# Row-wise infinity norm on one core: the second load moves to the first load's queue, and the last store goes out in two halves

## The chip, the core and the metric

The kernel runs on one core of a Trainium2 chip. The metric is the device time of one execution in microseconds (us), and lower is better. Three runs of the kernel before gave 629.17, 629.47 and 629.51, a median of 629.47.

A core has several engines with an instruction stream each. Three compute here: VectorE (DVE in the profile), ScalarE (ACT) and GpSimd (POOL). SyncE (SP) computes nothing and issues transfers. A transfer between the device's memory (HBM) and the on-chip memory of 128 partitions is issued by SP or by ScalarE's queue (ACTq), and is carried out by 16 DMA engines, whichever queue it came from. When it has landed, a semaphore tells those that wait for it.

## The reference

```python
def setup_inputs():
    return {"x": np.random.randn(8192, 8192).astype(np.float32)}

def reference(x):
    return np.linalg.norm(x, ord=np.inf, axis=1)
```

`x` is two-dimensional and an axis is given, so the norm is that of each row as a vector: the largest absolute value of its 8192 elements. The input has 268.4 MB, the output 32 KB.

## The kernel before

**Layout.** The 8192 rows are split over the 128 partitions, 64 rows in each, in two groups (`GROUPS = [46, 18]`): in a group of k rows per partition a partition's rows lie one behind the other in HBM. Along the free dimension the kernel walks through the 64 rows as one strip of 64 x 8192 values. A result column of the tile `res` (128 x 64) belongs to each of the 64 rows.

**Loads.** The strip is read by 38 loads. The list `WHOLE` has 31 of 16384 values per partition (two rows, 64 KB per partition, 8.39 MB in all) and one of 8192. The list `LAST` cuts the last row into six pieces of 3920, 1984, 1040, 576, 320 and 352 values. All but the last piece go into `ring`, which holds three whole loads; the last has a tile of its own (`last`), behind whose values the partial results of the last row are put. A load into a part of the ring that is in use waits until the work on it is done, so load 4 has to wait for the reduce of load 1, load 5 for that of load 2, and so on. For half the loads the kernel also declares that the wait for the earlier load itself isn't needed, since the reduces in between imply it.

**Reduces.** For every whole load VectorE runs one reduce over two rows with the maximum of absolute values (line 68, in the helper `absmax`). Towards the end, in the loads that have widths in their second entry, the work on a row is shared (helper `shared`): VectorE takes the first part, ScalarE takes the absolute values of the others (line 90), and GpSimd takes their maximum (line 75, helper `max_pool`), on the bits as integers. Another `max_pool` or, for the last row, a last `absmax` over 361 columns puts the partial results together.

**Queues.** The helper `load` issues every load by SP, except for the second one (`len(loads) == 1`), which ScalarE's queue issues (line 110). ScalarE's first computing instruction (line 142) has no effect on the results; it comes after the second load's reduce, and brings its table load to the front of ScalarE's stream.

**Stores.** SP issues the last store (`final`, line 156): the column of the last row, 128 x 1 values. ScalarE's queue issues two earlier ones (line 161): 46 columns of the first group and 17 of the second. The call of `add_manual_dep` behind them sets the order in which two of the stores get their semaphores; it adds no wait. At the end SP waits until all transfers have landed (line 192), and all engines meet.

`keep` fixes the order of what passes through it; the rest is ordered by the tile framework along the dependencies.

Of the kernel before, what the change touches and what calls it, by code (L numbers as in the profile page):

```python
# [1 line left out]

# [4 lines left out]

P = 128
FP32 = mybir.dt.float32
INT32 = mybir.dt.int32  # L10
MAX = mybir.AluOpType.max
X = mybir.AxisListType.X
ABS = mybir.ActivationFunctionType.Abs

GROUPS = [46, 18]


WHOLE = (
    [(16384, ())] * 30 + [(16384, (3712, 3680)), (8192, (2016, 1984))]
)
LAST = [
    (3920, (1680,)), (1984, (848,)), (1040, (432,)), (576, (240,)), (320, ()), (352, ())
]
RING = 3 * 16384


@with_exitstack  # L30
def kernel(
    ctx: ExitStack,
    tc: tile.TileContext,
    x: bass.AP,
    out: bass.AP,
):
    nc = tc.nc
    n_rows, n_cols = x.shape
    R = n_rows // P
    assert R == sum(GROUPS) and n_cols == 8192  # L40
    keep = tc.keep_in_program_order


    first = []
    x_of, out_of = {}, {}
    for k in GROUPS:
        f = len(first)
        x_of[f] = x[f * P : (f + k) * P].rearrange("(p r) m -> p (r m)", r=k)
        out_of[f] = out[f * P : (f + k) * P].rearrange("(p r) -> p r", r=k)
        first += [f] * k  # L50

    single = ctx.enter_context(tc.tile_pool(name="single", bufs=1))

    ring = single.tile([P, RING], FP32)
    res = single.tile([P, R], FP32)

    n_parts = sum(1 + len(g) for w, g in LAST[:-1])
    last = single.tile([P, LAST[-1][0] + n_parts], FP32)

    def not_before(inst, other, why):  # L60
        tc.add_manual_dep(
            inst.ins, other.ins.name,
            mybir.DependencyInfo(mybir.DependencyClass.Sync, mybir.DependencyReason.DATA),
            reason=why,
        )

    def absmax(dst, src):
        return keep(nc.vector.tensor_reduce(  # L68
            out=dst, in_=src, axis=X, op=MAX, apply_absolute_value=True,
        ))  # L70

    def max_pool(dst, src):

        pool = nc.gpsimd
        keep(pool.add_instruction(  # L75
            mybir.InstTensorReduce(
                name=nc.get_next_instruction_name(),
                ins=[pool.lower_ap(src.bitcast(INT32))],
                outs=[pool.lower_ap(dst.bitcast(INT32))],
                op=MAX,  # L80
                axis=X,
            )
        ))

    def shared(part, buf, g):

        a = buf.shape[1] - sum(g)
        red = absmax(part[:, :1], buf[:, :a])
        for i, c in enumerate(g):
            keep(nc.scalar.activation(buf[:, a : a + c], buf[:, a : a + c], ABS))  # L90
            max_pool(part[:, 1 + i : 2 + i], buf[:, a : a + c])
            a += c
        return red

    loads = []

    def load(pos, w):

        row = pos // n_cols
        a = pos - first[row] * n_cols  # L100
        if pos + w == R * n_cols:
            buf = last[:, :w]
        else:
            at = loads[-1][0] + loads[-1][1] if loads else 0
            if at + w > RING:
                at = 0
            buf = ring[:, at : at + w]

        queue = nc.scalar if len(loads) == 1 else nc.sync
        inst = queue.dma_start(out=buf, in_=x_of[first[row]][:, a : a + w]).ins  # L110
        if pos + w < R * n_cols:
            if (len(loads) + 4) % 10 < 5:


                for b, v, earlier in loads:
                    if b < at + w and at < b + v:
                        tc.declare_no_dep(
                            inst, earlier, reason="ordered by the reduces in between",
                        )
            loads.append((at, w, inst))  # L120
        return buf


    pos = 0
    for u, (w, g) in enumerate(WHOLE):
        buf = load(pos, w)
        row, k = pos // n_cols, w // n_cols
        pos += w
        whole = k - 1 if g else k
        if whole:  # L130
            red = absmax(
                res[:, row : row + whole],
                buf[:, : whole * n_cols].rearrange("p (c m) -> p c m", m=n_cols),
            )
        if g:
            part = single.tile([P, 1 + len(g)], FP32, name=f"part{u}")
            shared(part, buf[:, whole * n_cols :], g)
            max_pool(res[:, row + whole : row + k], part)
        if u == 1:

            not_before(
                keep(nc.scalar.activation(res[:, :1], res[:, :1], ABS)),  # L142
                red, "not before the second row is in",
            )


    n = LAST[-1][0]
    for h, (w, g) in enumerate(LAST[:-1]):
        buf = load(pos, w)
        pos += w  # L150
        shared(last[:, n : n + 1 + len(g)], buf, g)
        n += 1 + len(g)

    load(pos, LAST[-1][0])
    absmax(res[:, R - 1 :], last)
    final = nc.sync.dma_start(out=out_of[first[-1]][:, GROUPS[-1] - 1 :], in_=res[:, R - 1 :])


    for f, o in out_of.items():
        k = min(o.shape[1], R - 1 - f)  # L160
        early = keep(nc.scalar.dma_start(out=o[:, :k], in_=res[:, f : f + k]))
    tc.add_manual_dep(
        early.ins, final.ins.name,
        mybir.DependencyInfo(mybir.DependencyClass.NoSync, mybir.DependencyReason.SCHED_ONLY),
        reason="takes the later semaphore",
    )


# [1 line left out]
_INS = ['x']  # L170
_OUTS = [((8192,), 'float32')]


# [23 lines left out]
```

## Time and profile before

| | |
|---|---|
| runs of the kernel before | 629.17, 629.47, 629.51 us |
| the profiled execution, its own time | 629.51 us |
| its span in the profile | 627.7 us |
| HBM read, mean rate over the span | 268.44 MB, 428 GB/s |
| VectorE, wait for the first load | 41.9 us |
| VectorE, waits for loads in all | 89.2 us in 24 waits |
| SP's queue, share of 16 DMA engines | 260.05 MB, 96.0% |
| ScalarE's queue, share of 16 DMA engines | 8.42 MB, 3.1% |
| one reduce of a whole load, x31 with its other form | 16.94 us on average |

The span runs from the first to the last record of the profiled execution; its own time is 1.8 us longer. Engines are counted as busy while they compute, and the issue of a transfer isn't counted. A wait of VectorE for a load isn't a loss in itself where the DMA engines have no pause. The time to landing of a transfer counts from its issue and holds the time in which it stands in the queue behind others.

### The profile page before, as it was taken

The page shows a single profiled execution, that of the slowest core. Times are in us where ns is not written, and L with a number is a line of the kernel's source. Part 1 is how long each engine was busy: PE and PEld are TensorE (multiplying, and loading weights), DVE is VectorE, ACT ScalarE, POOL GpSimd, SP SyncE. Part 2 cuts the span into 40 slices and gives each one's busy share as a digit, 9 for nine tenths or more (in the row PEclk, how much of TensorE's full clock was granted, in tenths as well). Part 3 has the DMA queues.
Part 4 walks back from the last instruction along what each step waited for, and adds up shares of the span by engine and source line. Part 5 has one row for each costly group of instructions (what it writes and reads, how often), then busy time and mean ns, then how long its engine had stood idle before and what let it go on. Part 6 is the DMA issues. An engine that isn't in the chain of part 4 may idle for free.

```text
span 627.7 us, 173 instructions
## 1 busy us (share of the span) xinstructions
DVE 535.8 (85%) x39; ACT 15.0 (2%) x10; POOL 14.1 (2%) x14
## 2 busy tenths in 40 slices
DVE  0039999999998898888998888988889888899888
ACT  0000000000000000000000000000000000000044
POOL 0000000000000000000000000000000000000026
DMA  9999999999999999999999999999999999999996
GB/s 401 409 459 401 434 430 438 430 438 430 434 434 426 443 418 451 413 455 409 459 409 459 409 459 405 464 405 464 405 464 405 459 409 455 413 451 418 451 407 280
DMA packets 5904, 268.47 MB, mean 428 GB/s; under 512 B 1040, under 2 KB 1296, under 8 KB 1680
## 3 DMA queue, kind: packets, MB, share of 16 engines
q1 hardware_dynamic: 5472, 260.05, 96.0%
q10 hardware_dynamic: 432, 8.42, 3.1%
HBM read 268.44 MB, written 0.03 MB: 428 GB/s over the span
## 4 chain that ended last, share of the span: by engine, by line
DMA 57%; DVE 42%; issue 0%; SPq 0%; DVEq 0%
DMA ring<-in_x_dram 57%; DVE res L68 41%; DVE last L68 1%; SPq L110 0%; DVEq L68 0%
## 5 line engine op out<-in xcount | busy, mean ns | idle before, releaser
L68 DVE TENSOR_REDUCE res<-ring 128x2 f32<-128x16384 f32 (+1 forms) x31 | 524.6, 16942 | 89.2 <-DMA ring<-in_x_dram 89.2
L90 ACT ACTIVATE ring<-ring 128x3712 f32<-128x3712 f32 (+7 forms) x8 | 13.6, 1718 | 534.3 <-DMA ring<-in_x_dram 534.2
L75 POOL TENSOR_REDUCE part<-ring 128x1 int32<-128x3712 int32 (+3 forms) x4 | 10.1, 2562 | 609.7 <-ACT ring L90 609.7
L68 DVE TENSOR_REDUCE part<-ring 128x1 f32<-128x800 f32 (+1 forms) x2 | 5.5, 2748 | 0.1
L68 DVE TENSOR_REDUCE last<-ring 128x1 f32<-128x2240 f32 (+4 forms) x5 | 5.3, 1115 | 0.2 <-DMA ring<-in_x_dram 0.2
L75 POOL TENSOR_REDUCE last<-ring 128x1 int32<-128x1680 int32 (+3 forms) x4 | 3.4, 854 | 0.6 <-ACT ring L90 0.4
L142 ACT ACTIVATE res<-res 128x1 f32<-128x1 f32 x1 | 0.2, 203 | 73.8 <-DVE res L68 73.8
L142 ACT ACT_TABLE_LOAD x1 | 1.3, 1283 | 1.2 <-PEq L181 1.2
L68 DVE TENSOR_REDUCE res<-last 128x1 f32<-128x361 f32 x1 | 0.5, 530 | 0.1
L75 POOL TENSOR_REDUCE res<-part 128x1 int32<-128x3 int32 x2 | 0.4, 197 | 0.1
L181 POOL MEMSET const-float32-0.0<- 128x1 f32 x1 | 0.1, 98 | 0.2 <-issue 0.2
L181 POOL MEMSET const-bfloat16-1.0<- 128x1 bf16 x1 | 0.1, 101 | 0.0
L181 POOL MEMSET const-uint8-127<- 128x1 uint8 x1 | 0.1, 101 | 0.0
L181 POOL MEMSET const-float32-1.0<- 128x1 f32 x1 | 0.1, 98 | 0.0
## 6 DMA issues: line engine op xcount, KB each, us to landing
ring<-in_x_dram SPq DMA_DIRECT2D x1, 4096.0 KB, 31.1
ring<-in_x_dram SPq DMA_DIRECT2D x1, 1960.0 KB, 35.4
ring<-in_x_dram SPq DMA_DIRECT2D x1, 992.0 KB, 37.4
ring<-in_x_dram SPq DMA_DIRECT2D x1, 520.0 KB, 38.2
ring<-in_x_dram SPq DMA_DIRECT2D x30, 40.8
ring<-in_x_dram SPq DMA_DIRECT2D x1, 288.0 KB, 38.4
last<-in_x_dram SPq DMA_DIRECT2D x1, 176.0 KB, 38.3
ring<-in_x_dram SPq DMA_DIRECT2D x1, 160.0 KB, 38.3
```

Source lines behind the costliest of these rows:

```text
L68: return keep(nc.vector.tensor_reduce(out=dst, in_=src, axis=X, op=MAX, apply_absolute_value=True,))
L75: keep(pool.add_instruction(mybir.InstTensorReduce(name=nc.get_next_instruction_name(), ins=[pool.lower_ap(src.bitcast(INT32))], outs=[poo ...
L90: keep(nc.scalar.activation(buf[:, a : a + c], buf[:, a : a + c], ABS))
L142: keep(nc.scalar.activation(res[:, :1], res[:, :1], ABS)),
L181: nc = _bacc.Bacc("TRN2", target_bir_lowering=False, num_devices=1)
```

## The change

The second load is issued by SP, as all others are, so the rule by which a queue was chosen is gone. The last store is cut at partition 64: the upper half of the partitions goes by ScalarE's queue, behind the two earlier stores, and the lower half by SP. Each half waits for the last reduce. The call that sets the order of the semaphores now stands between these two.

```diff
-        queue = nc.scalar if len(loads) == 1 else nc.sync
-        inst = queue.dma_start(out=buf, in_=x_of[first[row]][:, a : a + w]).ins
+        inst = nc.sync.dma_start(out=buf, in_=x_of[first[row]][:, a : a + w]).ins
...
     load(pos, LAST[-1][0])
     absmax(res[:, R - 1 :], last)
-    final = nc.sync.dma_start(out=out_of[first[-1]][:, GROUPS[-1] - 1 :], in_=res[:, R - 1 :])
+    for f, o in out_of.items():
+        k = min(o.shape[1], R - 1 - f)
+        keep(nc.scalar.dma_start(out=o[:, :k], in_=res[:, f : f + k]))
 
 
-    for f, o in out_of.items():
-        k = min(o.shape[1], R - 1 - f)
-        early = keep(nc.scalar.dma_start(out=o[:, :k], in_=res[:, f : f + k]))
+    half = P // 2
+    o = out_of[first[-1]][:, GROUPS[-1] - 1 :]
+    second = keep(nc.scalar.dma_start(out=o[half:], in_=res[half:, R - 1 :]))
     tc.add_manual_dep(
-        early.ins, final.ins.name,
+        nc.sync.dma_start(out=o[:half], in_=res[:half, R - 1 :]).ins, second.ins.name,
         mybir.DependencyInfo(mybir.DependencyClass.NoSync, mybir.DependencyReason.SCHED_ONLY),
         reason="takes the later semaphore",
     )
```

## The prediction

> **What bounds the kernel now.** I read the page first (engine shares, the chain that ended last), then the chain in order of time, then single DMA issues with their landing times, and last the tail. Loads are numbered from 1 in the order of the code; load 2 is the one that ScalarE's queue issues.
>
> ```profile
> DVE 535.8 (85%) x39; ACT 15.0 (2%) x10; POOL 14.1 (2%) x14
> DMA  9999999999999999999999999999999999999996
> DMA 57%; DVE 42%; issue 0%; SPq 0%; DVEq 0%
> ```
>
> VectorE (DVE) is free for 15% of the span, while the DMA engines show 90% or more in all slices but the last. So data arrival should set the pace, although the chain gives VectorE 42%. The chain in time tells why it does:
>
> ```profile
> 0.74 41.12 DMA ring<-in_x_dram
> ...
> 41.88 137.11 DVE res L68 x8
> ...
> 179.01 39.12 DMA ring<-in_x_dram
> ...
> 218.16 17.23 DVE res L68
> ...
> 276.21 17.23 DVE res L68
> ...
> 566.47 17.23 DVE res L68
> ```
>
> Columns are start, length, what. From 218.16 on the chain repeats one pattern, a reduce of 17.23 and a load of 40.79, and VectorE waits 2.13 us before each reduce. The pace there is (566.47 - 218.16) / 18 loads = 19.35 us for 8.39 MB, with loads always queued behind each other. This is the stream's own pace. Two more readings stand against it. First, loads 1 and 2 land together, 41.12 us after their issue, which is 2 x 19.35 + 2.42: the start of the stream costs 2.42, and VectorE can't begin until 41.88. Second, from the landing of load 2 (41.86) to that of load 11 (218.13) nine loads take 176.27 us; nine at 19.35 would take 174.15. About 2.12 us are lost in there, although VectorE, which was late, isn't what a stream needs, unless it releases a buffer late. It does so once. The three rows below are from three looks: the issues near the start, the first reuse of a buffer (timeline), and that issue's time to landing.
>
> ```profile
> 0.73 0.40 ACTq L110 DMA_DIRECT2D ring<-in_x_dram  x1
> 0.74 0.85 SPq L110 DMA_DIRECT2D ring<-in_x_dram  x2
> DMA to landing us min/median/max: 41.1/41.3/60.0
> ```
>
> ```profile
> 59.13 0.33 SPq L110 DMA_DIRECT2D ring<-in_x_dram  x1
> ```
>
> ```profile
> ring<-in_x_dram SPq DMA_DIRECT2D x1, 23.6
> ```
>
> Load 3 is issued at about 1.17 and lands 60.0 later, at 61.2. Load 4 overwrites load 1's buffer, so it waits for the first reduce and is issued at 59.13, when only 2.0 us of load 3 are left in the queue. It lands at 59.13 + 23.6 = 82.7, that is 21.5 us after load 3 and not 19.35. The stream ran dry here, or nearly, and had to start again: 82.73 - 61.17 - 19.35 = 2.2 us lost, all of what the chain misses (2.12). Later issues have more cover; by 179.01 it is 39.12 - 19.35 = 19.8 us of queued loads, and nothing more is lost.
>
> The tail still hangs on arrival:
>
> ```profile
> 605.17 8.69 DVE L68 TENSOR_REDUCE res<-ring 128x1 f32<-128x8192 f32 x1 [2.13 <-DMA ring<-in_x_dram]
> 619.56 5.27 DVE L68 TENSOR_REDUCE last<-ring 128x1 f32<-128x2240 f32 x5 [0.16 <-DMA ring<-in_x_dram]
> 624.93 0.53 DVE L68 TENSOR_REDUCE res<-last 128x1 f32<-128x361 f32 x1
> 625.49 0.35 SPq L156 DMA_DIRECT2D out_dram<-res  x1
> ```
>
> VectorE waited for a load just before 605.17 and again before 619.56; from there it runs on to the last reduce (ends 625.46), SP issues the last store at 625.49, and the span ends at 627.7. If all loads come earlier by some amount, the tail from 605.17 comes earlier by as much, since 2.13 us of waiting stand before it and all of that is for loads.
>
> **The change part by part.**
>
> *Load 2 from ScalarE's queue to SP's, behind load 1.* ScalarE's queue loses one issue of 0.40 us; its table load (1.28 us from 1.16) moves up to about 0.74 and hides in 70 us of idle time. SP gains one issue: 0.33 to 0.43 by its own rows, before load 3, which then goes out near 1.6 instead of 1.17. At that time load 1 has 20 us to run, which hides it; without that cover it would cost 0.4. No wait is added: in the built order the first three SP loads wait for nothing, and the later waits are the old ones with load 1's and load 2's semaphores exchanged.
>
> What it does to the stream: load 1's packets no longer share the engines with load 2's. Load 1 then lands at 0.74 + 2.42 + 19.35 = 22.5 and load 2 still near 41.9, for the bytes are the same. The first reduce runs from 22.5 to 39.8, and load 4 is issued at 39.8 instead of 59.13, with 61.2 - 39.8 = 21.4 us of loads ahead of it. The steady part has the same cover (40.79 - 19.35 = 21.4) and loses nothing, so the dry spot goes: -2.12 by the chain, -2.2 by the two landings; I take -2.17. Where that stall goes: VectorE starts 19.4 us earlier, works off no backlog, and waits about 2.1 us for each load from the start. Loads are late next, at their own pace, and that nobody speeds up here. The gain isn't 19.4 us since a VectorE that starts early only waits more.
>
> Bounds on this term. The new start is one queue's alone, which no row shows cold. The nearest rows are the cold start of the two queues (2.42 from issue) and load 4's lone issue, which lands 23.6 - 19.35 = 4.25 after it, 2.0 of them behind load 3. Were the whole 4.25 the price of a lone start, it would cost 4.25 - 2.42 = 1.8 and leave -0.35. The other end: a lone issue takes 0.33 instead of 0.38 and, without the second queue, the start might lose 0.3 less, giving -2.5. I stay at 2.42 because it is the only start from rest in the trace. A queue with three whole loads also is no new thing: before the end SP has eight loads issued and not landed (the issues up to 586.47 stand behind a load that lands near 605).
>
> *The last store in two halves.* One SP issue of 0.35 us and 128 rows becomes two issues of 64 rows, on SP and on ScalarE's queue, both waiting for the last reduce. ScalarE's half stands behind two stores that end at 624.32 + 0.44 = 624.77, 0.7 us before the reduce is done; behind it is only the engine's end. SP's half gets another earlier semaphore to wait for, that of the load reduced at 621.97, long landed. The rows for such a store:
>
> ```profile
> out_dram<-res ACTq DMA_DIRECT2D x1, 23.0 KB, 1.5
> out_dram<-res ACTq DMA_DIRECT2D x1, 8.5 KB, 1.5
> out_dram<-res SPq DMA_DIRECT2D x1, 0.5 KB, 1.4
> ```
>
> Forty-six times the bytes cost 0.1 us, so halving the bytes gains 0 to 0.1. Against it, ScalarE's rows are 0.1 longer than SP's, and two issues at once took 0.40 and 0.38 at the start where a lone one takes 0.33. If the second half's issue waits out the first it costs 0.35; if the halves go wholly one after the other, 1.4. I take +0.1, bounds -0.1 and +1.4, nearest to the pair at the start, whose landings (41.1 and 41.3) lie within 0.2.
>
> A rule of the Trainium skill speaks against this part: the page "DMA: Bandwidth & Descriptors", section "Rules for kernel authors", says not to split a transfer into two partition halves, because both use the same 16 engines and serialize. The rows above agree that loads share the engines, and leave open what it means for 256 bytes. With that page's fixed cost of about 2 us for a DMA (its section on the anatomy of a DMA, given there for another issuing path) a full serialization would be an estimated 629.3 in place of 627.4.
>
> Sum on the profiled execution: 629.51 - 2.17 + 0.1 = 627.44 (span 627.7 - 2.07 = 625.6, and 1.8 around it). The median of the runs shown is 629.47, 0.04 below that execution: 627.4.
>
> **The rivals.**
>
> *A slow lone start.* Load 1 lands near 24.3 instead of 22.5. For it: load 4's lone issue took 4.25. Against: part of that was spent behind load 3, and load 4 had to wait for engines still busy. Time: 629.47 - 0.35 + 0.1 = 629.2.
>
> *The halves serialize.* For it: the second store on ScalarE's queue needed 0.44 where the one ahead took 0.34. Against: the two loads at the start went on together. Time: 629.47 - 2.17 + 1.4 = 628.7.
>
> *The change doesn't do what it says*: load 1 lands no earlier because the engines take loads 1 and 2 in turn even from one queue, so load 4 still goes out near 59. Against it: from load 4 on each SP load lands 19.35 after the one before, never in pairs. Time: 629.47 + 0.1 = 629.6.
>
> *Slower: one late DMA engine.* A load is landed when the last of its engines is done, and engines that take their shares from one queue don't wait for each other. If the lone cold start leaves one of them behind, every later landing is behind by as much, to the end. It is priced at its lag, one for one; it makes the kernel slower than before from 2.07 us of lag beyond today's start, and measurably so from 2.07 + 1.26 = 3.3; with 3.6 it is 631.0. For it: the loss at load 4 stayed to the end. Against: both starts seen lie 1.8 apart at most.
>
> **How the numbers follow.** 0.2% is 1.26 us, about what a measurement of this kernel tells from no change: faster is below 628.21. Gap closed, 627.4: 0.74, by itself 626.9 to 628.0. Slow lone start, 629.2: 0.10, a third of it still under 628.21. Halves serialize, 628.7: 0.07, a quarter of it under. No effect, 629.6: 0.04. Late engine, 631.0: 0.05. Faster 0.74 + 0.03 + 0.02 = 0.79; slower 0.05 and 0.01 from the top of the no-effect case; same 0.15. Range 626.7 to 628.8: below, the -2.5 and a store gain of 0.1; above, up to the serialized halves.
>
> **What would show it.** First reduce near 22.5; load 4 issued near 40 and landing 19.35 after load 3, about 41 after its issue; a wait of 2.13 before each reduce from the second on; the last reduce ending near 623.3; two stores issued together, landing within 0.2 of each other about 1.5 later. Wrong would be a landing of load 1 past 24, any two loads over 20 us apart, or an end more than 2.4 us after the last reduce.

## The result, and the profile after

The changed kernel took 628.0 us (median of 6 runs, 627.92 to 628.12), the kernel before 630.0 (median of 6 runs: the three shown above, 629.17 to 629.51, and three beside the changed kernel, 630.49 to 631.1). The ratio is 0.9967 with a 95% interval of 0.9954 to 0.998: 0.33% faster, between 0.2% and 0.46%. Run again later against other runs of the kernel before, the changed kernel had a ratio of 0.9977 (0.9968 to 0.9986). The profiled execution took 627.92, with a span of 626.1 against 627.7.

The page of the changed kernel, engine shares and the chain that ended last:

```profile
DVE 536.5 (86%) x39; ACT 15.0 (2%) x10; POOL 14.1 (2%) x14
DMA 71%; DVE 28%; SPq 0%; issue 0%; DVEq 0%
```

VectorE does the same work in the same time, but the chain's share of it fell from 42% to 28%: the long stretch of eight reduces in a row, in which VectorE caught up, is gone. The same chain in order of time (start, length, what):

```profile
0.74 0.38 SPq L108
...
1.18 40.68 DMA ring<-in_x_dram
41.85 0.02 issue
41.88 17.23 DVE res L68
59.11 0.02 issue
59.12 40.79 DMA ring<-in_x_dram
...
564.36 17.23 DVE res L68
```

From 41.88 on, the pattern of one reduce and one load repeats to the end: (564.36 - 41.88) / 27 loads = 19.35 us, the stream's own pace, now without an exception. The timeline around the first reuse of a buffer, in rows from three windows:

```profile
22.56 17.22 DVE L68 TENSOR_REDUCE res<-ring 128x2 f32<-128x16384 f32 x1 [22.56 <-DMA ring<-in_x_dram]
39.80 0.33 SPq L108 DMA_DIRECT2D ring<-in_x_dram  x1
61.23 17.22 DVE L68 TENSOR_REDUCE res<-ring 128x2 f32<-128x16384 f32 x1 [2.13 <-DMA ring<-in_x_dram]
80.59 17.22 DVE L68 TENSOR_REDUCE res<-ring 128x2 f32<-128x16384 f32 x1 [2.15 <-DMA ring<-in_x_dram]
```

Load 1 is there at 22.56 instead of 41.88, load 4 goes out at 39.80 instead of 59.13, and the reduces of loads 3 and 4 (the last two rows) start 19.36 apart. Before, load 4 landed 21.5 after load 3.

The tail (timeline), and the last two stores' times from issue to landing:

```profile
617.44 5.28 DVE L68 TENSOR_REDUCE last<-ring 128x1 f32<-128x2240 f32 x5 [0.16 <-DMA ring<-in_x_dram]
622.82 0.53 DVE L68 TENSOR_REDUCE res<-last 128x1 f32<-128x361 f32 x1
623.38 0.53 SPq L163 DMA_DIRECT2D out_dram<-res  x1
623.38 0.54 ACTq L161 DMA_DIRECT2D out_dram<-res  x1
```

```profile
out_dram<-res SPq DMA_DIRECT2D x1, 0.2 KB, 1.7
out_dram<-res ACTq DMA_DIRECT2D x1, 0.2 KB, 2.0
```

The last reduce starts 2.11 us earlier than before (624.93), all of it won at the front. It ends at 623.35 and the span at 626.1: 2.8 us, where the kernel before needed 627.7 - 625.46 = 2.3. So the store gives 0.5 back. Each half takes 0.53 to issue, where the whole store took 0.35, and lands 1.7 and 2.0 later instead of 1.4. The sum, -2.1 + 0.5, is the -1.6 of the two spans.

### The profile page after: what moved, and what is told of

Read it like the earlier page. It is cut to its first block, busy times and chain, and to the rows that moved or that the text cites. A ratio compares the mean times of both kernels' runs of the same rounds, so it can differ in the third digit from the quotient of the medians.

```text
span 626.1 us, 174 instructions
## 1 busy us (share of the span) xinstructions
DVE 536.5 (86%) x39; ACT 15.0 (2%) x10; POOL 14.1 (2%) x14
## 4 chain that ended last, share of the span: by engine, by line
DMA 71%; DVE 28%; SPq 0%; issue 0%; DVEq 0%
DMA ring<-in_x_dram 71%; DVE res L68 28%; DVE last L68 1%; SPq L108 0%; DVEq L68 0%
```

## The experiments

Each is a kernel of its own; medians are given with the range of their runs. A ratio compares with runs of the kernel before on the same chip, taken together with the row's own. The first four rows share one chip, the next four another, and e5 and e6 a third.

| kernel | us, median (range) | ratio to before (95%) |
|---|---|---|
| load 2 by SP, old store (e1) | 627.52 (627.38 to 627.67) | 0.9973 (0.9963 to 0.9984) |
| load 2 by ScalarE, store in halves (e2) | 629.85 (629.04 to 630.38) | 1.0010 (1.0001 to 1.0019) |
| e1, load 4 held back until the second reduce is done (e3) | 629.28 (628.57 to 630.53) | 1.0005 (0.9997 to 1.0014) |
| before, load 4 in two pieces (e4) | 627.52 (627.37 to 627.69) | 0.9976 (0.9965 to 0.9986) |
| the changed kernel again (a1) | 628.02 (627.95 to 628.21) | 0.9977 (0.9968 to 0.9986) |
| e1, whole store by ScalarE's queue (s3) | 627.53 (627.33 to 627.57) | 0.9969 (0.9956 to 0.9981) |
| both halves by SP (s4) | 628.45 (628.31 to 628.58) | 0.9985 (0.9976 to 0.9994) |
| e1, 17 columns stored beside the last store (s5) | 627.77 (627.64 to 628.22) | 0.9973 (0.9964 to 0.9983) |
| e1, load 4 held back until half of the second reduce is done (e5) | 627.50 (627.38 to 627.69) | 0.9970 (0.9958 to 0.9983) |
| e1, load 4 held back until 15/16 of the second reduce are done (e6) | 628.05 (627.62 to 629.50) | 0.9980 (0.9971 to 0.9989) |

Two more kernels, s6 and s7, ran once each, on the chip of e5 and e6, for the issue times in their profiles; their total times are not used.

### The two parts alone (e1, e2)

e1 keeps the load part and restores the old store; e2 keeps `nc.scalar if len(loads) == 1 else nc.sync` and has the new store.

```diff
 # e1, against the changed kernel
+    final = nc.sync.dma_start(out=out_of[first[-1]][:, GROUPS[-1] - 1 :], in_=res[:, R - 1 :])
...
-    second = keep(nc.scalar.dma_start(out=o[half:], in_=res[half:, R - 1 :]))
...
```

> Load 2 by SP as in the changed kernel, last store whole by SP as before. Theory (a dry spot before load 4 cost some 2.1 us, the halved store gives 0.5 back): last reduce starts near 622.8 as in the changed kernel, last store lands 1.4 after its issue, span 625.6, time 627.4, that is 0.5 below the changed kernel's 627.9 to 628.1. Rival (the 0.5 that the forecast missed belongs to the front and not to the store): span 626.1, time 628.0, and the store takes as long as in the changed kernel.

> Load 2 stays on ScalarE's queue, the last store in two halves. Theory: slower than before by 0.5 us (about 630.0 where before has 629.5), both halves issued together with about 0.53 us each. Rival (the halves cost nothing by themselves): no difference from before, issues of 0.35.

e1 measured 627.52, 0.3% faster than before, and e2 was slower than before by 0.1% (0.01% to 0.19%), some 0.6 us. The tail of e1 (timeline):

```profile
623.05 0.53 DVE L68 TENSOR_REDUCE res<-last 128x1 f32<-128x361 f32 x1
623.61 0.35 SPq L154 DMA_DIRECT2D out_dram<-res  x1
```

Its span of 625.9 ends 2.3 us after the reduce, as before the change. The gain is the load's and the loss the store's, and e1 beats both kernels. Side by side on one chip, the changed kernel took 628.02 (a1) and s3, which differs from it in the store alone, 627.53: the store in halves costs 0.5.

### The dry spot (e3, e4)

Was it load 4's late issue that cost the time, or do two queues reading at once slow the stream? e3 uses one queue and makes load 4 late; e4 uses two queues and gets load 4 out in time, by reducing load 1 row by row and loading the next buffer in two pieces.

```diff
 # e3, against e1
+        if len(loads) == 3:
+            tc.add_manual_dep(inst, reds[1].ins.name, ...)   # waits for the second reduce
...
 # e4, against before
-    [(16384, ())] * 30 + [(16384, (3712, 3680)), (8192, (2016, 1984))]
+    [(16384, ())] * 3 + [(8192, ())] * 2 + [(16384, ())] * 26 + [(16384, (3712, 3680)), (8192, (2016, 1984))]
...
+            step = 1 if u == 0 else whole
...
```

> As the run with load 2 by SP and the old store, but load 4 also waits for the second reduce, so it goes out near 59.1 instead of 39.8 although no second queue is used. Theory (what cost time was the late issue of load 4): load 4 lands over 21 us after load 3, the loss of 2 us or more is back, the time is within 0.6 us of before's. Rival (two queues reading at once are slower by themselves): nothing is lost, 627.4.

> The kernel before with load 2 still on ScalarE's queue and the old store, but the first reduce works row by row and load 4 comes in two pieces of one row each, so that its first piece goes out near 50.5 with some 10 us of load 3 ahead of it. Theory: loads 1 and 2 still land together near 41.9, yet the stream doesn't run dry and 2 us are gained, 627.4 to 627.6. Rival (two queues at once are slower by themselves): as before, 629.5 or more.

The timeline of e3, issue of load 4 and the reduces of loads 3 and 4:

```profile
59.09 0.81 SPq L109 DMA_DIRECT2D ring<-in_x_dram  x2
...
61.18 17.22 DVE L68 TENSOR_REDUCE res<-ring 128x2 f32<-128x16384 f32 x1 [2.12 <-DMA ring<-in_x_dram]
82.11 17.22 DVE L68 TENSOR_REDUCE res<-ring 128x2 f32<-128x16384 f32 x1 [3.71 <-DMA ring<-in_x_dram]
```

Without any second queue the two are 20.93 apart, 1.6 more than the pace, and e3 took as long as the kernel before. In the chain of e4,

```profile
0.74 41.34 DMA ring<-in_x_dram
42.10 137.24 DVE res L68 x10
179.36 36.95 DMA ring<-in_x_dram
```

VectorE starts as late as in the kernel before, at 42.10, and works off the same backlog in ten reduces. Its timeline has the first piece of load 4 leaving at 50.81:

```profile
50.81 0.33 SPq L110 DMA_DIRECT2D ring<-in_x_dram  x1
```

The load that the chain has from 179.36 on lands at 216.31; the kernel before had it at 218.13. So e4 has the whole gain, 627.52, the same as e1. Two queues by themselves cost nothing here (e4), and an early VectorE by itself brings nothing (e3). What moved the time is when load 4 is issued.

### How early is early enough (e5, e6)

Both have one queue, and load 4 waits for part of the second reduce: for the first of its two rows in e5, for 15/16 of its values in e6 (the reduce is cut there and put together by a small one over two columns).

```diff
 # e5: the second load's reduce row by row, and load 4 waits for reds[1], its first row
+            step = 1 if u == 1 else whole
...
 # e6: load 4 waits for the second of these
+                cut = n_cols + 7168
+                absmax(res[:, row : row + 1], buf[:, :n_cols])
+                reds.append(absmax(two[:, :1], buf[:, n_cols:cut]))
...
```

> Load 2 by SP, old store; the second reduce works row by row and load 4 waits for its first row, so it goes out near 50.6, with 10 us of load 3 ahead of it. Theory (a load that goes out late costs nothing as long as its first data comes before the queue is empty): 19.35 between the landings of loads 3 and 4, 627.5. Rival (each microsecond of lateness behind 39.8 costs a part of the 1.7 that the fully late load 4 cost, in proportion): 628.4.

> The same with load 4 waiting for 15/16 of the second reduce, so that it goes out near 58.1 with about 3 us of load 3 ahead of it, 1 us earlier than in the kernel before. Theory: all 16 engines have the first descriptors some 2.7 us after the issue, as load 4's packets in the kernel before show, so 3 us are just enough, 19.4 to 19.8 between loads 3 and 4, 627.5 to 627.9. Rival (the loss falls in step with the cover): half of the 1.7 is left, 628.3.

The timeline of e5:

```profile
50.83 0.33 SPq L109 DMA_DIRECT2D ring<-in_x_dram  x1
...
61.48 17.22 DVE L68 TENSOR_REDUCE res<-ring 128x2 f32<-128x16384 f32 x1 [2.08 <-DMA ring<-in_x_dram]
80.83 17.22 DVE L68 TENSOR_REDUCE res<-ring 128x2 f32<-128x16384 f32 x1 [2.13 <-DMA ring<-in_x_dram]
```

Its load 4 left 11 us later than in the changed kernel, with some 10.6 us of load 3 still to come, and e5 took 627.50: this lateness cost nothing. In e6's timeline

```profile
58.22 1.45 SPq L109 DMA_DIRECT2D ring<-in_x_dram  x2
...
61.33 17.22 DVE L68 TENSOR_REDUCE res<-ring 128x2 f32<-128x16384 f32 x1 [1.81 <-DMA ring<-in_x_dram]
81.40 17.22 DVE L68 TENSOR_REDUCE res<-ring 128x2 f32<-128x16384 f32 x1 [2.86 <-DMA ring<-in_x_dram]
```

the issue stands 3.1 us before load 3 is seen, and the two reduces are 20.07 apart: 0.7 lost in this execution, 0.55 by the medians against e5, and up to 2.0 in one of 11 runs. So 3 us aren't enough; 628.05 lies between the expected range, which ended at 627.9, and the rival's 628.3. With about 2.1 us of cover e3 lost 1.8 against e1, by their medians on one chip; with 10 us nothing is lost. Where between 3 and 10 the loss ends wasn't tried.

The packet records of the traces tell more of this loss than "dry" does. A packet here is one partition's 64 KB, and each of the 16 DMA engines moves eight of them per load, in 2.42 us each as a rule. In the kernel before, the engines stood still for 0.4 us on average between load 3 and load 4, and then the first packet of load 4 took 2.7 to 3.6 us, 0.7 more than 2.42 on average. In e6 no engine stood still, but the first packet took 2.7 to 3.1 us on three of the 16, and this alone is the 0.7 of its profile. In e5 and the changed kernel all of them took 2.42. Why first packets are slow when a load is issued so late, no run shows.

### Why a halved store is slow (a1, s3, s4, s5, s6, s7)

```diff
 # s3: the last store whole, by ScalarE's queue, in place of the halves
...
+    keep(nc.scalar.dma_start(out=out_of[first[-1]][:, GROUPS[-1] - 1 :], in_=res[:, R - 1 :]))
 # s4: both halves by SP
-    second = keep(nc.scalar.dma_start(out=o[half:], in_=res[half:, R - 1 :]))
+    second = keep(nc.sync.dma_start(out=o[half:], in_=res[half:, R - 1 :]))
 # s5: as e1, ScalarE's store of 17 columns waits for the last reduce (end)
...
+    not_before(early, end, "together with the last store")
```

> The changed kernel once more, beside the variants of its last store on the same chip. Theory: 627.9 to 628.1, two issues at once of 0.53 each, landings of 1.7 and 2.0, against 0.35 and 1.4 for the whole store by SP (627.5 in the run with load 2 moved alone).

> Load 2 by SP, last store whole (128 rows), issued by ScalarE's queue alone. Theory (two issues at the same time slow each other): an issue of 0.35 to 0.44 and a landing of 1.4 to 1.6, 627.5 to 627.7. Rival (a store on ScalarE's queue lands late whatever runs beside it): landing of 2.0, 628.0 or more.

> Load 2 by SP, both halves of the last store issued by SP, one behind the other. Theory (two issues at the same time slow each other): the first issue takes 0.35, the second 0.35 to 0.44, the second lands 0.4 later than a whole store would, 627.9 to 628.0. Rival (a store of 64 rows is slower to issue than one of 128): the first issue already takes 0.5 or more, time 628.1 or more.

> Load 2 by SP, last store whole by SP, but the store of 17 columns on ScalarE's queue waits for the last reduce too, so that two stores of 128 rows are issued at once. Theory (two issues at the same time slow each other, whatever their shape): both issues take 0.5 or more, landings of 1.7 to 2.0, 628.0. Rival (it is the shape of 64 rows): issues of 0.35 to 0.4, 627.6.

The theory was that two issues at the same time slow each other. It fell twice. In the timeline of s4 the first issue of SP has nothing beside it and still takes 0.53; in that of s5 two stores of 128 rows go out at once and take 0.34 and 0.37. The third timeline is that of s3:

```profile
623.34 0.53 SPq L161 DMA_DIRECT2D out_dram<-res  x1
623.90 0.59 SPq L163 DMA_DIRECT2D out_dram<-res  x1
```

```profile
623.56 0.34 SPq L154 DMA_DIRECT2D out_dram<-res  x1
623.56 0.37 ACTq L159 DMA_DIRECT2D out_dram<-res  x1
```

```profile
623.33 0.34 ACTq L157 DMA_DIRECT2D out_dram<-res  x1
```

Nor is ScalarE's queue to blame: in s3 it issues the whole store in 0.34, and s3's 627.53 is as good as e1's 627.52 on its chip. (s5 is 0.2 above s3: its store of 17 columns, which the end now waits for, lands 1.7 after its issue.) It is the store of 64 rows itself that takes 0.53 to issue. The issues of s4 and s5, from issue to landing:

```profile
out_dram<-res SPq DMA_DIRECT2D x2, 0.2 KB, 1.7
```

```profile
out_dram<-res SPq DMA_DIRECT2D x1, 0.5 KB, 1.4
out_dram<-res ACTq DMA_DIRECT2D x1, 8.5 KB, 1.7
```

The halves of s4 land 1.7 after their issue, 0.3 later than a whole store, and 0.18 of that is the longer issue. Being issued together adds a second part, some 0.2 on ScalarE's side: its half in the changed kernel lands after 2.0, and its store of 17 columns in s5 after 1.7, where the same store took 1.5 in the kernel before. No run tells what this second part is. Issued one behind the other, s4 loses 0.43 more than the changed kernel.

Two kernels cut ScalarE's two earlier stores, s6 by rows (64 and 64, 32 and 96) and s7 by columns (23 and 23, 8 and 9, all 128 rows).

```diff
 # s6, by rows
+        cuts = [(0, 64), (64, 128)] if f == 0 else [(0, 32), (32, 128)]
+        for p, q in cuts:
+            early = keep(nc.scalar.dma_start(out=o[p:q, :k], in_=res[p:q, f : f + k]))
 # s7, by columns
+        early = keep(nc.scalar.dma_start(out=o[:, : k // 2], in_=res[:, f : f + k // 2]))
+        early = keep(nc.scalar.dma_start(out=o[:, k // 2 : k], in_=res[:, f + k // 2 : f + k]))
```

> Load 2 by SP, last store whole by SP; the store of 46 columns goes as two of 64 rows, that of 17 columns as 32 and 96 rows, all on ScalarE's queue. Theory (a store of fewer than 128 rows takes longer to issue, whatever its bytes): the first issue takes about 0.53, the others 0.5 to 0.6, against 0.38 and 0.44 for the two of 128 rows. Rival (only the one-column store is slow in halves): 0.38, then 0.44 for each. The time is of no use here, the four stores end behind the last one.

> The same four stores cut by columns instead, 23, 23, 8 and 9 columns with all 128 rows. Theory (the rows count): 0.38 for the first and 0.44 for those behind it. Rival (a store of half the bytes or an offset in the tile is what is slow): 0.5 or more for the second and the fourth. The time is of no use here either.

Their timelines, the first with 64, 64, 32 and 96 rows in this order:

```profile
622.01 0.54 ACTq L161 DMA_DIRECT2D out_dram<-res  x1
622.59 0.61 ACTq L161 DMA_DIRECT2D out_dram<-res  x1
623.24 0.60 ACTq L161 DMA_DIRECT2D out_dram<-res  x1
623.87 0.44 ACTq L161 DMA_DIRECT2D out_dram<-res  x1
```

```profile
622.03 0.38 ACTq L159 DMA_DIRECT2D out_dram<-res  x1
622.44 0.45 ACTq L160 DMA_DIRECT2D out_dram<-res  x1
622.92 0.45 ACTq L159 DMA_DIRECT2D out_dram<-res  x1
623.41 0.45 ACTq L160 DMA_DIRECT2D out_dram<-res  x1
```

Cut by columns, the stores keep 0.38 for the first and 0.45 for those behind another. With 64 or 32 rows each takes about 0.15 more, whatever its columns. The 96 rows, at 0.44, are as quick as 128, so "fewer rows are slower", as expected of s6, is wrong too. Row counts of 32 and 64 are slow here, 96 and 128 aren't, with one store each of 32 and of 96 rows; what lies behind that is open.

## Why the prediction was right, and where it wasn't

**The bound and the dry spot: right.** That arrival sets the pace, that VectorE's share of the chain was backlog, and that load 4's late issue let the stream run dry are what e3, e4 and e5 show, each by moving that issue (e4 and e5 also cut one reduce in two, and e4 load 4). Every sign named for it came: the first reduce at 22.56 (22.5 forecast), load 4 out at 39.80 (39.8), then 19.36 to the next landing, a wait of 2.1 before each reduce.

**Its size: right in the profile, a little smaller in the runs.** -2.17 was taken, and the last reduce came 2.11 earlier between the two profiled executions. Between the medians of e1 and of the kernel before it is 1.5 us, by their ratio 1.7 (1.0 to 2.3). The size isn't fixed: in 27 runs on one chip the kernel before ranged from 628.60 to 630.73, while e1 and e4, without a dry spot, stayed within 0.3. The trace's packet records show one cause. Times at which the first and the last of the 16 DMA engines were done with a load:

| kernel | load 3 | load 4 | load 30 |
|---|---|---|---|
| before | 60.34 to 60.85 | 80.47 to 82.38 | 583.43 to 585.35 |
| changed | 60.38 to 60.87 | 79.72 to 80.20 | 582.78 to 583.24 |
| load 2 by ScalarE, store in halves (e2) | 60.43 to 60.79 | 80.59 to 81.33 | 583.56 to 584.34 |

In the profiled execution of the kernel before, the first engine to be done lost 0.8 between loads 3 and 4 (80.47 - 60.34 - 19.35), the last one 2.2, and the last was as far behind the first at load 30. In e2, with the same loads, the last one lost 1.2. So what the prediction called a late engine exists, but in the old kernel. And "ran dry" was the smaller part of the loss: 0.4 us of idle engines on average, against 0.7 in the slow first packets of load 4, which the prediction didn't have. The lone cold start, priced between 1.8 worse and 0.3 better, was as good as the old one: the engines lie 0.5 apart in both.

**The store: the term that was mis-sized.** The step "I take +0.1 ... nearest to the pair at the start" should have been +0.5. The row it chose was a pair of 128-row loads. That pair showed no price of being issued together, since the first load of the changed kernel, issued alone, takes 0.38 as well, and s5 shows that a pair of 128-row stores isn't slow to issue. The trace of before had no transfer of 64 rows, so no row priced the issue of one. The sum of 627.44 for the profiled execution against 627.92 measured is almost all this; the median of 628.0 against 627.4 is it too, with the smaller gain at the front.

**The ratio: luck.** The forecast of 627.4 for 629.47 is a ratio of 0.9967, and that is exactly what was measured. Two misses cancel in it: the store cost 0.4 more than forecast, and the kernel before took 630.49 to 631.1 in the three runs beside the changed one, above the 629.47 that the forecast started from. On the three chips of the experiments its median was 629.06 to 629.38, and the changed kernel's ratio on one of them 0.9977.

**Two readings that were loose.** The landing at 41.86 is that of load 1; load 2, by ScalarE's queue, landed 41.3 after 0.73, at 42.03. The nine loads up to load 11 then miss 1.95 and not 2.12, while the 2.2 between loads 3 and 4 stands. And the lower end of the range adds up to 629.47 - 2.5 - 0.1 = 626.9, not 626.7. Neither moves the forecast time by more than 0.1.

**The rivals.** "Slow lone start" and "no effect" are out by the first reduce at 22.56 and by load 4. "The halves serialize", with +1.4, is out in that form: even one behind the other by SP they cost 628.45 - 627.53 = 0.9. It was the nearest to the truth in direction, and the forecast's own sign of error, an end more than 2.4 us after the last reduce, did show up with 2.8. The rule of the Trainium skill that was weighed there (page "DMA: Bandwidth & Descriptors", section "Rules for kernel authors") is right in its advice for this case. Its reason, shared engines, is at most a part of what was measured: of the 0.5 lost, some 0.3 come with a half that is issued with nothing beside it (s4), 0.18 of them in the issue. The other 0.2 come only when the two are issued together; whether shared engines are behind that, no run shows.

## What to carry to other kernels

Where a stream of loads sets the end, look for two neighbouring landings that are further apart than the others and for the issue that came too late; here about 10 us of queued loads were enough and 3 weren't. An earlier start of the engine that consumes the loads was worth what it did for the next issue and no more (e3). Before splitting a small last transfer, look for a transfer of that shape in a trace: here such a store cost 0.5 more and saved nothing. The load part alone, with the old store, gives 627.52.

## What was not expected

Stores of 64 and 32 rows took 0.53 to 0.61 us to issue, those of 96 and 128 rows 0.34 to 0.45, whatever the bytes. A lag that the DMA engines got against each other at load 4 wasn't made up: in the kernel before it was 1.9 us there and still at load 30. And 3 us between an issue and the end of the queued loads still lost 0.55 us by the median, and in one of 11 runs 2.0; in the profiled execution no engine stood still, and the loss was in slow first packets.
